# Weight-quarter sums of a Strassen product moved from GpSimd to VectorE, in three additions with changed signs

## The chip, the cores and the metric

The kernel runs on one core of a Trainium2 chip. The metric is the device time of one execution in microseconds, the median of the timed runs. The engines are named as the profile names them: PE is the matrix engine, TensorE (PEld its weight loads), DVE is VectorE, ACT is ScalarE, POOL is GpSimd, SP issues the transfers.

## The reference

Four residual layers work on x of 512 tokens by 1024 features, in float32. Layers 0 and 3 mix tokens with a gated short convolution, layer 1 with a spatial-gating unit (SGU), layer 2 with retention; each is followed by a SwiGLU feed-forward network (FFN) of 2816 hidden features, and a last RMSNorm closes.

```python
for i in range(4):
    h = rmsnorm(x, norm_mix_g[i])
    x = x + mixer[i % 3](h)                    # conv, SGU, retention, conv
    h = rmsnorm(x, norm_ffn_g[i])
    x = x + (silu(h @ w_gate) * (h @ w_up)) @ w_down
return rmsnorm(x, final_norm_g)

# the convolution mixer
b_gate, c_gate, z = split(h @ w_in, 3)
m = (b_gate * causal_conv3(c_gate * z)) @ w_out
```

## The kernel before

All activations lie with features on the 128 partitions and tokens along the row. Every float32 operand of a product is split into two float32r tiles whose sum it is (`split`, L156: ACT casts the high part, L157, then DVE subtracts it from the source to get the low part, L158), and a product is the three matmuls high by high, high by low, low by high (`product`, L177).

The products that read the residual stream in the convolution and FFN layers (`columns7`, L205) are made by Winograd's form of Strassen's product: weights and activations are cut into 2 by 2 quarters, and seven products of quarters or of sums of quarters take the place of eight. Each product is 12 matmuls of 256 columns, so a chunk of weights (two blocks of 128 output features) is 84 matmuls. Results are gathered from PSUM by short ACT copies (L227, L229, L233, L243) and DVE additions (`add`, L224).

`prepare7` (L114) makes the left operands of one chunk, in two halves of 512 KB each. For each half SP issues a transfer into a `raw` tile; the four sums of its quarters go into a `sums` tile, three of them by POOL in a chain (L131, L132, L133) and one by DVE (L134); then the three quarters that are used as they are, 128x768, and the four sums, 128x1024, are split by ACT and DVE. `weights` prepares at most one such chunk ahead of the one in use. `raw` has four buffers, `sums` two, the split weights four.

On the side of the activations, `operand_sums` (L382) makes the four sums of quarters for each pair of feature blocks: two by DVE (L391, L393) and two by POOL (L392, L394), then splits them (tiles th and tl). It runs once for each of the four pairs wherever a layer ends whose successor uses `columns7`. `operand` (L366) makes the plain parts xh and xl (L374, L375), and `squares` (L295) sums the squares of the new x on POOL (L302 to L307).

An FFN runs its hidden features in four parts. In a part of three pairs six chunks follow each other (gate, up, gate, up, ...; the tiles pg and pu), each 84 matmuls; within the next part's first pair the part's down projection (`leave`, L402) is added to x, eight blocks of 512-column matmuls. The first chunk of a layer is made by `columns4`, which needs no sums of the activations.

The order on each engine is made when the program is built, by a scheduler that simulates the engines; instructions marked urgent (`high_priority`) may pass up to 100 others. Each engine executes its own list strictly in that order.

Of the kernel before, what the change touches and what calls it, by code (L numbers as in the profile page):

```python
# [11 lines left out]
F32 = mybir.dt.float32  # L12
F32R = mybir.dt.float32r
# [4 lines left out]
P = 128  # L18
D = 1024
T = 512  # L20
DEPTH = 4
NB = D // P            # feature blocks of the residual stream
NT = T // P            # token blocks
FF = 2816
NF = FF // P
H = T // 2             # tokens of half the sequence
FF_PARTS = ((0, 2), (2, 5), (5, 8), (8, 11))  # pairs of hidden blocks, by part of an FFN
# [8 lines left out]
LAG = 3                # blocks of u that are ahead of the mixing of v  # L36
SOON = 100             # instructions that urgent ones may pass in the scheduler's order
BEGUN = 4              # blocks whose products begin before the last of their operands are ready
AHEAD = 4              # weight chunks prepared ahead of their matmuls


class Kernel:
# [19 lines left out]
    def dense(self):  # L62
        """Memory of the layers whose products take seven parts."""
# [10 lines left out]
    @contextmanager  # L74
    def mixed(self):
        """Memory of the other layers."""
        with self.tc.tile_pool(name="blk", bufs=29, reuse_waits="tile") as self.blk:
            yield

# [17 lines left out]
    def plan7(self, src, plain=False):  # L97
        """Two blocks of columns, for columns4 if plain, else for columns7."""
        self.chunks.append((src, 0, plain))
# [14 lines left out]
    def prepare7(self, i):  # L114
        """Two blocks of columns, as the seven left operands of Winograd's form of Strassen's product."""
# [3 lines left out]
        for half in range(2):  # L119
            raw = self.raw.tile([P, NB // 4, 4, P], F32, tag="raw", name=f"raw{i}{half}")  # L120
            nc.sync.dma_start(raw, src[half])
            if plain:
                h, l = (self.wp.tile([P, NB // 4, 4, P], F32R, tag=part, name=f"w{part}{i}{half}") for part in "hl")
                self.split(raw, h, l)
                for j in range(4):
                    out[j] += [(h[:, k, j], l[:, k, j]) for k in range(NB // 4)]
                continue
            sums = self.sums.tile([P, NB // 4, 4, P], F32, tag="sums", name=f"sums{i}{half}")
            a11, a12, a22, a21 = (raw[:, :, j] for j in range(4))
            s1, s2, s3, s4 = (sums[:, :, j] for j in range(4))  # L130
            nc.gpsimd.tensor_add(s1, a21, a22)  # L131
            nc.gpsimd.tensor_sub(s2, s1, a11)  # L132
            nc.gpsimd.tensor_sub(s4, a12, s2)  # L133
            nc.vector.tensor_sub(s3, a11, a21)  # L134
            for x, n, first, pool in ((raw, 3, 0, self.w7), (sums, 4, 3, self.wp)):
                h, l = (pool.tile([P, NB // 4, n, P], F32R, tag=part, name=f"w{part}{i}{half}{n}") for part in "hl")
                self.split(x[:, :, :n], h, l)
                for j in range(n):
                    out[first + j] += [(h[:, k, j], l[:, k, j]) for k in range(NB // 4)]
# [15 lines left out]
    def split(self, src, h, l):  # L155
        """A float32 tile as two float32r tiles whose sum it is."""  # L156
# [9 lines left out]
    def product(self, ps, terms, first=True, last=True, more=False):  # L166
        """ps (+)= sum of lhsT.T @ rhs over (lhs_h, lhs_l, rhs_h, rhs_l), the last term's at the end;
        more: added to a finished sum."""
# [12 lines left out]
    def columns(self, name, acts):  # L181
        """One block of output features (on partitions), for all tokens."""
# [14 lines left out]
    def begin(self, name, acts):  # L197
        """The start of columns(), with the weights of the rest."""
# [5 lines left out]
    def columns7(self, name, then, hold=False):  # L204
        """Two blocks of output features of the residual stream. then() gets them as [P, 2 * T], when the  # L205
        next product is under way."""
# [21 lines left out]
        part(c5, 3, xt, 0, True)  # L228
# [3 lines left out]
        part(c1, 4, xt, 1, False)  # L232
# [5 lines left out]
        part(c1, 5, xt, 2, False)  # L238
        add(y[:, 2 * H : 3 * H], c1, m5)

        def end():
            part(c1, 2, xt, 3, False)
            nc.scalar.copy(y[:, 3 * H :], c1)  # L243
# [4 lines left out]
    def columns4(self, name, then, hold=False):  # L248
        """The same by four products of blocks, for which the sums of the operand needn't be ready."""
# [16 lines left out]
    def finish(self, hold=False):  # L266
        """The rest of the last columns7, and what is done with its outcome (and those before it) unless on hold."""
# [8 lines left out]
    def rows(self, name, acts):  # L276
        """512 output features for each block of tokens (on partitions)."""
# [17 lines left out]
    def squares(self, src, add=None):  # L295
        """Running sum, over feature blocks, of the squares."""
# [12 lines left out]
    def rsqrt(self, ps, out, t):  # L309
        """out = ps ** -0.5, with a Newton step."""  # L310
# [7 lines left out]
    def scale_of(self, mean, r, t, *sums):  # L318
        """Each token's 1 / rms, on all partitions."""
# [8 lines left out]
    def diagonal(self, eye):  # L328
        """The matrix that mean_d is the inverse of, on vectors: D on the diagonal."""
# [8 lines left out]
    def scale_of_tokens(self, total):  # L338
        """Each token's 1 / rms, with tokens on partitions: a column for 128 of them."""
# [12 lines left out]
    def spread(self, r, t):  # L352
        """The same on all partitions, in PSUM."""
# [7 lines left out]
    def scale_in_psum(self):  # L361
        """Each token's 1 / rms, on all partitions."""
        return self.spread(self.scale_of_tokens(self.sum), self.hid.tile([P, 2 * T], F32, tag="hid", name="rs")[:, :T])

# [1 line left out]
    def operand(self, m, g):  # L366
        """x's block m as a part of the next product's operand."""
# [592 lines left out]
```

## Time and profile before

| what | value |
|---|---|
| median of 3 runs | 2485.07 us (2484.79 to 2485.66) |
| span of the profiled execution | 2484.2 us |
| PE busy | 2417.6 us, 97% |
| DVE busy | 1836.7 us, 74%, 2236 instructions |
| ACT busy | 1132.3 us, 46% |
| POOL busy | 890.0 us, 36%, 788 instructions |

The span runs from the first to the last instruction of one profiled execution. No separate time of that execution is given beside its span; the median of the timed runs is 0.9 us above it. A busy share is an average over stages with different limits: the seven-part stages (convolution and FFN) and the SGU and retention layers between them load DVE and POOL quite differently.

### The profile page before, as it was taken

Reading aid. Unit: us, or ns where it says so; the run is one execution under the profiler, and the core shown is the slowest. Engines: PE = TensorE matmul, PEld = TensorE weight load, DVE = VectorE, ACT = ScalarE, POOL = GpSimd, SP = SyncE. Lnnn points to the kernel's source line nnn. Section 1 sums busy time; section 2 is a strip of 40 time slices with the busy share of each in tenths; the row PEclk is TensorE's granted clock in tenths of the full one; section 3 lists DMA queues with packets and bytes.
Section 4 is the critical chain, followed back from the end, with each engine's and each line's share of the span. In section 5 each row is a group of like instructions: output and inputs, shape, how many; then the busy total and the mean of one; then the engine's idle time right before and its main releaser. Section 6 shows DMA issues by size and latency. Waiting matters only on the chain.

```text
span 2484.2 us, 37622 instructions
## 1 busy us (share of the span) xinstructions
PE 2417.6 (97%) x14892; PEld 2179.7 (88%) x14892; DVE 1836.7 (74%) x2236; ACT 1132.3 (46%) x1638; POOL 890.0 (36%) x788
## 2 busy tenths in 40 slices
PE   7999999999999999999999999999999899999998
PEld 6988989988888899998888888799999788889988
DVE  7988878763757887767565465988767898978776
ACT  6455445443324544534333334545435545545443
POOL 5536533520101643442000000834433744733530
PEclk9999999999999999999999999999999999999999
DMA  4141333334332233233223131233234124133231
GB/s 154 62 145 53 116 111 95 97 115 119 94 103 92 68 111 122 88 97 122 95 72 94 60 123 58 91 107 115 85 98 132 52 69 153 52 119 103 85 112 59
DMA packets 78832, 242.09 MB, mean 97 GB/s; under 512 B 8768, under 2 KB 12864, under 8 KB 78656
## 3 DMA queue, kind: packets, MB, share of 16 engines
q1 hardware_dynamic: 77568, 238.65, 30.3%
q8 instruction: 116, 1.90, 0.3%
q10 hardware_dynamic: 1088, 1.05, 0.1%
q14 instruction: 60, 0.49, 0.1%
HBM read 237.56 MB, written 2.10 MB: 96 GB/s over the span
## 4 chain that ended last, share of the span: by engine, by line
PE 75%; DVE 16%; issue 5%; ACT 2%; POOL 1%; DMA 0%; SPq 0%; DVEq 0%; ACTq 0%; POOLq 0%
PE out L177 26%; PE pu L177 16%; PE pg L177 15%; PE pv L177 7%; DVE wl L158 6%; PE pc L177 2%; PE q L177 2%; PE k L177 2%; PE pb L177 2%; DVE sums L134 2%; DVE puy L512 1%; PE pz L177 1%; DVE xl L375 1%; PE po L177 1%; DVE pgy L488 1%
## 5 line engine op out<-in xcount | busy, mean ns | idle before, releaser
L157 ACT CAST wh<-raw 128x768 fp32r<-128x768 f32 (+3 forms) x500 | 425.1, 858 | 572.5 <-PE out L177 193.5
L158 DVE TENSOR_TENSOR wl<-raw,wh 128x768 fp32r<-128x768 f32 (+3 forms) x500 | 557.6, 1134 | 136.7 <-ACT wh L157 136.3
L131 POOL TENSOR_TENSOR sums<-raw 128x256 f32<-128x256 f32 x208 | 243.3, 1170 | 795.8 <-DMA raw<-in_ffn_w_up 360.7
L157 ACT CAST wh<-sums 128x1024 fp32r<-128x1024 f32 x208 | 212.2, 1046 | 182.6 <-POOL sums L133 78.0
L177 PE MATMUL out<-hidl,wh 128*128 128x512 f32 (+1 forms) x736 | 278.3, 380 | 0.0
L158 DVE TENSOR_TENSOR wl<-sums,wh 128x1024 fp32r<-128x1024 f32 x208 | 260.9, 1279 | 22.1 <-ACT wh L157 18.8
L177 PE MATMUL out<-hidh,wh 128*128 128x512 f32 (+1 forms) x736 | 274.6, 381 | 0.0
L133 POOL TENSOR_TENSOR sums<-raw,sums 128x256 f32<-128x256 f32 x208 | 230.1, 1107 | 10.4
L132 POOL TENSOR_TENSOR sums<-sums,raw 128x256 f32<-128x256 f32 x208 | 217.9, 1048 | 10.6
L177 PE MATMUL pg<-xl,wh 128*128 128x256 f32 (+1 forms) x672 | 201.9, 316 | 9.6 <-DVE xl L375 9.6
L422 DVE TENSOR_TENSOR x<-out,x 128x512 f32<-128x512 f32 x192 | 130.2, 683 | 107.0 <-PE out L177 105.9
L177 PE MATMUL out<-hidh,wl 128*128 128x512 f32 (+1 forms) x736 | 205.4, 380 | 0.0
L177 PE MATMUL pg<-xh,wh 128*128 128x256 f32 (+1 forms) x672 | 200.9, 315 | 0.0
L177 PE MATMUL pu<-tl,wh 128*128 128x256 f32 x704 | 185.4, 284 | 5.1 <-DVE tl L158 5.1
L177 PE MATMUL pu<-xl,wh 128*128 128x256 f32 (+1 forms) x656 | 190.0, 306 | 0.0
L177 PE MATMUL pu<-xh,wh 128*128 128x256 f32 (+1 forms) x656 | 189.7, 306 | 0.0
L134 DVE TENSOR_TENSOR sums<-raw 128x256 f32<-128x256 f32 x208 | 153.3, 752 | 44.1 <-DMA raw<-in_ffn_w_up 37.9
L177 PE MATMUL pu<-th,wh 128*128 128x256 f32 x704 | 185.5, 285 | 0.0
L177 PE MATMUL pg<-th,wh 128*128 128x256 f32 x640 | 168.3, 284 | 6.9 <-DVE pgy L224 6.9
L177 PE MATMUL pg<-tl,wh 128*128 128x256 f32 x640 | 167.3, 283 | 0.0
L177 PEld LDWEIGHTS out<-hidl,wh 128*128 128x128 f32 x736 | 138.6, 188 | 25.1
L177 PEld LDWEIGHTS out<-hidh,wh 128*128 128x128 f32 x736 | 137.8, 188 | 25.0
(261 smaller groups left out, 6064.5 us busy)
## 6 DMA issues: line engine op xcount, KB each, us to landing
raw<-in_ffn_w_gate SPq DMA_DIRECT2D x88, 512.0 KB, 3.6
raw<-in_ffn_w_up SPq DMA_DIRECT2D x88, 512.0 KB, 3.6
raw<-in_ffn_w_down SPq DMA_DIRECT2D x96, 384.0 KB, 3.3
raw<-in_conv_w_in SPq DMA_DIRECT2D x48, 512.0 KB, 3.7
raw<-in_sgu_w_v SPq DMA_DIRECT2D x16, 512.0 KB, 3.6
raw<-in_sgu_w_u SPq DMA_DIRECT2D x16, 512.0 KB, 3.5
raw<-in_sgu_w_out SPq DMA_DIRECT2D x16, 512.0 KB, 3.5
raw<-in_ret_w_qk SPq DMA_DIRECT2D x16, 512.0 KB, 3.6
```

The lines of the kernel that those rows point to most:

```text
L131: nc.gpsimd.tensor_add(s1, a21, a22)
L132: nc.gpsimd.tensor_sub(s2, s1, a11)
L133: nc.gpsimd.tensor_sub(s4, a12, s2)
L134: nc.vector.tensor_sub(s3, a11, a21)
L157: self.nc.scalar.copy(h, src)
L158: self.nc.vector.tensor_sub(l, src, h.bitcast(F32))
L177: nc.tensor.matmul(ps, x, y, start=first and i == 0, stop=last and i == len(seq) - 1, skip_group_check=more)
L375: nc.vector.scalar_tensor_tensor(l[:, s], x[:, s], gm, h[:, s].bitcast(F32), ALU.mult, ALU.subtract)
L422: nc.vector.tensor_add(x[:, s], ps, x[:, s])
L488: self.nc.vector.tensor_mul(y, y, r.unsqueeze(1).broadcast_to([P, 2, T]))
L512: nc.vector.tensor_mul(y[:, s], y[:, s], g[:, s])
```

## The change

The signs of the sums are chosen so that all four sums of weight quarters are pure sums. They are made by DVE alone, in three additions: one of 512 columns that adds the fourth quarter, broadcast, to the first and third, and two of 256 columns that each add a quarter to the sum before. The opposite signs go to the activations: `operand_sums` makes its two chained sums on DVE as scalar_tensor_tensor instructions, and two results of `columns7` are negated where they are read out. The quarters lie one behind the other in a tile (the weights are laid out so in memory), and the slots of the four sums change their order. Comments are left out below.

```diff
-            raw = self.raw.tile([P, NB // 4, 4, P], F32, tag="raw", name=f"raw{i}{half}")
-            nc.sync.dma_start(raw, src[half])
...
-            sums = self.sums.tile([P, NB // 4, 4, P], F32, tag="sums", name=f"sums{i}{half}")
-            a11, a12, a22, a21 = (raw[:, :, j] for j in range(4))
-            s1, s2, s3, s4 = (sums[:, :, j] for j in range(4))
-            nc.gpsimd.tensor_add(s1, a21, a22)
-            nc.gpsimd.tensor_sub(s2, s1, a11)
-            nc.gpsimd.tensor_sub(s4, a12, s2)
-            nc.vector.tensor_sub(s3, a11, a21)
+            raw = self.raw.tile([P, 4, NB // 4, P], F32, tag="raw", name=f"raw{i}{half}")
+            sums = self.sums.tile([P, 4, NB // 4, P], F32, tag="sums", name=f"sums{i}{half}")
+            nc.sync.dma_start(raw, src[half])
+            nc.vector.tensor_add(sums[:, :2], raw[:, 3:].broadcast_to([P, 2, NB // 4, P]), raw[:, :3:2])
+            nc.vector.tensor_add(sums[:, 2], sums[:, 1], raw[:, 0])
+            nc.vector.tensor_add(sums[:, 3], sums[:, 2], raw[:, 1])
...
-        part(c5, 3, xt, 0, True)
+        part(c5, 4, xt, 0, True)
...
-        part(c1, 4, xt, 1, False)
+        part(c1, 5, xt, 1, False)
...
-        part(c1, 5, xt, 2, False)
-        add(y[:, 2 * H : 3 * H], c1, m5)
+        part(c1, 3, xt, 2, False)
+        with self.tc.high_priority(SOON):
+            nc.vector.scalar_tensor_tensor(y[:, 2 * H : 3 * H], c1, -1.0, m5, ALU.mult, ALU.subtract)
...
-            nc.scalar.copy(y[:, 3 * H :], c1)
+            nc.scalar.mul(y[:, 3 * H :], c1, -1.0)
...
-        nc.vector.tensor_sub(t1, b12, b11)
-        nc.gpsimd.tensor_sub(t2, b22, t1)
+        nc.vector.tensor_sub(t1, b11, b12)
         nc.vector.tensor_sub(t3, b22, b12)
-        nc.gpsimd.tensor_sub(t4, b21, t2)
+        nc.vector.scalar_tensor_tensor(t2, t1, -1.0, b22, ALU.mult, ALU.subtract)
+        nc.vector.scalar_tensor_tensor(t4, t2, -1.0, b21, ALU.mult, ALU.subtract)
```

In the changed program the lines below L115 stand one lower: the three additions of weight quarters are L132, L133 and L134, `operand_sums` is L392 to L395, the result with the changed sign is L240.

The change moves instructions at three places. The first is DVE's list within a part of the first FFN, from the split of one chunk's sums to the next chunk's. In the names the first two digits are the chunk, the next its half: wl5804 is the low part of the sums of half 0 of chunk 58, wl5803 that of its plain quarters. Before:

```order
L158 TENSOR_TENSOR wl5804_4107<-sums580_4097,wh5804_4106 128x1024
L158 TENSOR_TENSOR wl5814_4122<-sums581_4112,wh5814_4121 128x1024
L134 TENSOR_TENSOR sums590_4228<-raw590_4226 128x2x128
L134 TENSOR_TENSOR sums591_4243<-raw591_4241 128x2x128
L158 TENSOR_TENSOR wl5803_4103<-raw580_4095,wh5803_4102 128x768
L158 TENSOR_TENSOR wl5813_4118<-raw581_4110,wh5813_4117 128x768
L488 TENSOR_TENSOR pgy_4042<-pgy_4042,rps_2337 128x1024
```

And in the change, from the first addition for chunk 59 on:

```order
L132 TENSOR_TENSOR sums590_4181<-raw590_4180 128x512
L132 TENSOR_TENSOR sums591_4195<-raw591_4194 128x512
L158 TENSOR_TENSOR wl5803_4058<-raw580_4051,wh5803_4057 128x768
L133 TENSOR_TENSOR sums590_4181<-sums590_4181,raw590_4180 128x256
L158 TENSOR_TENSOR wl5813_4072<-raw581_4065,wh5813_4071 128x768
L489 TENSOR_TENSOR pgy_3998<-pgy_3998,rps_2313 128x1024
L133 TENSOR_TENSOR sums591_4195<-sums591_4195,raw591_4194 128x256
L224 TENSOR_TENSOR puy_4127<-pu2_4081,pum_4082 128x256
L134 TENSOR_TENSOR sums590_4181<-sums590_4181,raw590_4180 128x256
L224 TENSOR_TENSOR puy_4127<-pu5_4080,pum_4083 128x256
L134 TENSOR_TENSOR sums591_4195<-sums591_4195,raw591_4194 128x256
```

Two instructions for a chunk's sums have become six, and the two halves take turns, with other work between the links of each half's chain.

The second place is the end of DVE's list of the third FFN, where the activations for the second convolution are made after the last addition to x: xl2, xl3 and tl2, tl3 are the low parts for the last two pairs of feature blocks, xt their sums. Before:

```order
L375 SCALAR_TENSOR_TENSOR xl2_18033<-x2_90,gain_92,xh2_18032 128x512 x2
L134 TENSOR_TENSOR sums3121_18248<-raw3121_18246 128x2x128
L158 TENSOR_TENSOR tl2_18079<-xt_18071,th2_18078 128x1024
L391 TENSOR_TENSOR xt_18133<-xg_18132 128x256
L393 TENSOR_TENSOR xt_18133<-xg_18132 128x256
L375 SCALAR_TENSOR_TENSOR xl3_18107<-x3_91,gain_92,xh3_18106 128x512 x2
L158 TENSOR_TENSOR tl3_18141<-xt_18133,th3_18140 128x1024
```

In the change:

```order
L134 TENSOR_TENSOR sums3121_18100<-sums3121_18100,raw3121_18099 128x256
L395 SCALAR_TENSOR_TENSOR xt_17927<-xt_17927,xg_17926 128x256
L158 TENSOR_TENSOR tl1_17855<-xt_17847,th1_17854 128x1024
L376 SCALAR_TENSOR_TENSOR xl2_17889<-x2_90,gain_92,xh2_17888 128x512 x2
L392 TENSOR_TENSOR xt_17989<-xg_17988 128x256
L393 TENSOR_TENSOR xt_17989<-xg_17988 128x256
L394 SCALAR_TENSOR_TENSOR xt_17989<-xt_17989,xg_17988 128x256
L158 TENSOR_TENSOR tl2_17935<-xt_17927,th2_17934 128x1024
L395 SCALAR_TENSOR_TENSOR xt_17989<-xt_17989,xg_17988 128x256
L376 SCALAR_TENSOR_TENSOR xl3_17963<-x3_91,gain_92,xh3_17962 128x512 x2
L158 TENSOR_TENSOR tl3_17997<-xt_17989,th3_17996 128x1024
```

Between the last addition to x and tl3 DVE had 13 instructions and now has 21: the sums that POOL made (L394, L395) and the additions of weight quarters stand among them.

The third place is PE's list in the first convolution, at the matmul `scale` that sums the squares over the features (pc1 and pc2 are PSUM tiles of the products around it). Before, `scale` is row 153 of PE's list:

```order
L177 MATMUL pc2_466<-xh0_112,wh303_358 128x256
L344 MATMUL scale_496<-mean_d_94,sum_336 128x1 x4
L177 MATMUL pc2_466<-xl0_113,wh303_358 128x256
L177 MATMUL pc2_466<-xh1_119,wh303_358 128x256
L177 MATMUL pc2_466<-xl1_120,wh303_358 128x256
```

In the change it is row 208:

```order
L177 MATMUL pc1_460<-tl2_319,wh314_375 128x256
L177 MATMUL pc1_460<-th0_294,wl304_362 128x256
L345 MATMUL scale_492<-mean_d_94,sum_336 128x1 x4
L177 MATMUL pc1_460<-th1_306,wl304_362 128x256
L177 MATMUL pc1_460<-th2_318,wl314_376 128x256
```

The sum of squares is now asked for 55 rows of PE's list later, behind more products of 256 columns.

## Rows read from the trace of the kernel before

**Rows 1.** The page: span, and busy time of each engine.

```profile
span 2484.2 us, 37622 instructions
...
PE 2417.6 (97%) x14892; PEld 2179.7 (88%) x14892; DVE 1836.7 (74%) x2236; ACT 1132.3 (46%) x1638; POOL 890.0 (36%) x788
```

**Rows 2.** The waits view: engine, line waited for, us in total, times, longest.

```profile
ACT th L157 <- POOL xt L394: 31.3, 15, 3.8
...
PE pg L177 <- DVE xl L375: 9.6, 8, 2.8
...
PE pg L177 <- DVE pgy L224: 6.9, 9, 0.9
...
PE pu L177 <- DVE tl L158: 5.1, 3, 2.6
...
PE scale L344 <- DVE sum L307: 5.0, 1, 5.0
...
PE pc L177 <- DVE xl L375: 4.5, 3, 2.3
```

**Rows 3.** PE's timeline between two chunks of the first FFN: start, us, operation, idle before.

```profile
413.59 0.39 PE L177 MATMUL pg<-th,wh 128*128 128x256 f32 x1 [0.75 <-DVE pgy L224]
413.81 0.28 PE L177 MATMUL pg<-tl,wh 128*128 128x256 f32 x1
413.93 0.28 PE L177 MATMUL pg<-th,wh 128*128 128x256 f32 x1
```

**Rows 4.** DVE's timeline in the first FFN: start, us, operation, number joined.

```profile
360.20 0.42 DVE L134 TENSOR_TENSOR sums<-raw 128x256 f32<-128x256 f32 x1
...
362.77 0.96 DVE L158 TENSOR_TENSOR wl<-raw,wh 128x768 fp32r<-128x768 f32 x1
...
380.69 2.35 DVE L158 TENSOR_TENSOR wl<-sums,wh 128x1024 fp32r<-128x1024 f32 x2
382.96 1.85 DVE L134 TENSOR_TENSOR sums<-raw 128x256 f32<-128x256 f32 x2
384.74 2.90 DVE L158 TENSOR_TENSOR wl<-raw,wh 128x768 fp32r<-128x768 f32 x2
387.56 1.76 DVE L512 TENSOR_TENSOR puy<-puy,pgy 128x1024 f32<-128x1024 f32 x1
...
398.44 1.21 DVE L488 TENSOR_TENSOR pgy<-pgy,rps 128x1024 f32<-128x1024 f32 x1
...
402.24 1.22 DVE L158 TENSOR_TENSOR wl<-sums,wh 128x1024 fp32r<-128x1024 f32 x1
```

**Rows 5.** POOL's timeline in the same stretch, two rows of twelve.

```profile
383.72 0.81 POOL L132 TENSOR_TENSOR sums<-sums,raw 128x256 f32<-128x256 f32 x1
...
385.37 1.45 POOL L133 TENSOR_TENSOR sums<-raw,sums 128x256 f32<-128x256 f32 x1
```

**Rows 6.** DVE's timeline where the third FFN ends and the second convolution begins.

```profile
1918.65 0.68 DVE L422 TENSOR_TENSOR x<-out,x 128x512 f32<-128x512 f32 x1
1919.25 0.74 DVE L375 SCALAR_TENSOR_TENSOR xl<-x,gain,xh 128x512 fp32r<-128x512 f32 x1
...
1934.56 1.21 DVE L158 TENSOR_TENSOR tl<-xt,th 128x1024 fp32r<-128x1024 f32 x1
...
1940.32 1.51 DVE L134 TENSOR_TENSOR sums<-raw 128x256 f32<-128x256 f32 x1
...
1948.66 1.65 DVE L158 TENSOR_TENSOR tl<-xt,th 128x1024 fp32r<-128x1024 f32 x1 [0.57 <-ACT th L157]
```

**Rows 7.** The windows view: window, length, busy of PE, PEld, DVE, ACT, POOL, PEclk, DMA, GB/s.

```profile
51.00:57.00 6.00, 5.76 (x27) 5.79 (x28) 5.39 (x9) 0.96 (x3) 5.69 (x6) 0.50 0.01 2
1925.00:1975.00 50.00, 43.14 (x275) 38.26 (x274) 42.76 (x47) 30.20 (x45) 37.28 (x33) 0.97 0.14 43
1975.00:2080.00 105.00, 97.52 (x748) 93.38 (x747) 94.02 (x116) 48.83 (x83) 50.22 (x41) 1.00 0.29 93
```

**Rows 8.** Groups by line and form: busy, mean ns of one, idle before and its releasers.

```profile
L134 DVE TENSOR_TENSOR sums<-raw 128x256 f32<-128x256 f32 x208 | 153.3, 752 | 44.1 <-DMA raw<-in_ffn_w_up 37.9 <-DMA raw<-in_conv_w_in 5.0
```

More of the change, by code (lines that the diff above doesn't have):

```diff
@@ L119, in prepare7 @@
         for half in range(2):
-            raw = self.raw.tile([P, NB // 4, 4, P], F32, tag="raw", name=f"raw{i}{half}")
-            nc.sync.dma_start(raw, src[half])
             if plain:
-                h, l = (self.wp.tile([P, NB // 4, 4, P], F32R, tag=part, name=f"w{part}{i}{half}") for part in "hl")
+                raw = self.raw.tile([P, 4, NB // 4, P], F32, tag="raw", name=f"raw{i}{half}")
+                nc.sync.dma_start(raw, src[half])
+                h, l = (self.wp.tile([P, 4, NB // 4, P], F32R, tag=part, name=f"w{part}{i}{half}") for part in "hl")
                 self.split(raw, h, l)
                 for j in range(4):
-                    out[j] += [(h[:, k, j], l[:, k, j]) for k in range(NB // 4)]
+                    out[j] += [(h[:, j, k], l[:, j, k]) for k in range(NB // 4)]
                 continue
-            sums = self.sums.tile([P, NB // 4, 4, P], F32, tag="sums", name=f"sums{i}{half}")
-            a11, a12, a22, a21 = (raw[:, :, j] for j in range(4))
-            s1, s2, s3, s4 = (sums[:, :, j] for j in range(4))
-            nc.gpsimd.tensor_add(s1, a21, a22)
-            nc.gpsimd.tensor_sub(s2, s1, a11)
-            nc.gpsimd.tensor_sub(s4, a12, s2)
-            nc.vector.tensor_sub(s3, a11, a21)
+            raw = self.raw.tile([P, 4, NB // 4, P], F32, tag="raw", name=f"raw{i}{half}")
+            sums = self.sums.tile([P, 4, NB // 4, P], F32, tag="sums", name=f"sums{i}{half}")
+            nc.sync.dma_start(raw, src[half])
+            nc.vector.tensor_add(sums[:, :2], raw[:, 3:].broadcast_to([P, 2, NB // 4, P]), raw[:, :3:2])
+            nc.vector.tensor_add(sums[:, 2], sums[:, 1], raw[:, 0])
+            nc.vector.tensor_add(sums[:, 3], sums[:, 2], raw[:, 1])
             for x, n, first, pool in ((raw, 3, 0, self.w7), (sums, 4, 3, self.wp)):
-                h, l = (pool.tile([P, NB // 4, n, P], F32R, tag=part, name=f"w{part}{i}{half}{n}") for part in "hl")
-                self.split(x[:, :, :n], h, l)
+                h, l = (pool.tile([P, n, NB // 4, P], F32R, tag=part, name=f"w{part}{i}{half}{n}") for part in "hl")
+                self.split(x[:, :n], h, l)
                 for j in range(n):
-                    out[first + j] += [(h[:, k, j], l[:, k, j]) for k in range(NB // 4)]
+                    out[first + j] += [(h[:, j, k], l[:, j, k]) for k in range(NB // 4)]
         return out
@@ L880, in columns_by_two @@
     n, k, m = w.shape
-    w = w.reshape(n, 2, k // (4 * P), 2, P, m // (2 * P), 2, P).transpose(0, 5, 1, 4, 2, 6, 3, 7)
-    return np.ascontiguousarray(w.reshape(n, m // (2 * P), 2, P, k // (4 * P), 4, P)[..., [0, 1, 3, 2], :])
+    w = w.reshape(n, 2, k // (4 * P), 2, P, m // (2 * P), 2, P).transpose(0, 5, 1, 4, 6, 3, 2, 7)
+    return np.ascontiguousarray(w.reshape(n, m // (2 * P), 2, P, 4, k // (4 * P), P)[:, :, :, :, [0, 1, 3, 2]])
 def columns_first(w, parts=1):
```

## The prediction

> **What bounds the kernel now.** First the page: PE is busy for 97% of the span, DVE for 74%, POOL for 36% [rows 1]. The matmuls are the same before and after, so what can be won is PE's idle time and the stretches in which its clock is low, and what can be lost is new idle time. A matmul of 256 columns starts 0.12 us after the one before it [rows 3], so a chunk of 84 takes 10.08 us and a pair of chunks (gate and up) 20.16 us; no change of DVE or POOL makes that shorter.
>
> Next the waits. Those of PE that end with DVE are few [rows 2]: 9.6 and 4.5 us for the plain parts xl and 5.1 us for tl, all where a layer hands over to a layer of seven-part products; 6.9 us in nine pieces for pgy, within the FFNs; 5.0 us in one piece for the sum of squares at the first `scale`. Together 31.1 us. After the wait for `scale` the granted clock is 0.50, the lower level of 1.2 GHz, through 6 us [rows 7]: 3 us of PE's work at full speed are lost there. So 34 us is about all that faster handing over could give, and only the places of these waits matter.
>
> Then DVE's timeline, to see why it is late there. In the first FFN a pair of chunks takes DVE from 380.69 to 402.24, 21.55 us [rows 4], more than PE's 20.16. DVE falls behind by some 1.4 us a pair, and PE waits when the slack of a part is used up: the row of 0.75 us for pgy is that wait [rows 3]. DVE is slow there because of POOL. The addition of 256 columns takes 0.42 us when POOL rests and the split of 768 columns 0.96; while POOL works on sums [rows 5], two of the first take 1.85 and two of the second 2.90, and an addition of 1024 columns 1.76 where it takes 1.21 alone [rows 4]. The next operation starts about 0.08 us before the end of the one in front (2.35 for two splits that start 1.13 apart), so I count 0.34, 0.60, 0.88 and 1.13 us for 256, 512, 768 and 1024 columns: the 512 is from x's addition, which is followed after 0.60 us [rows 6]. A slowed operation costs (1.85 - 0.84) / 2, about 0.54 us more, counted at the starts: 0.89 for 0.34, 1.42 for 0.88.
>
> **The change, part by part.**
>
> *Weight sums in an FFN.* A pair holds two chunks, four halves. Removed per pair: twelve POOL additions, and with them the delay of four additions (4 x 0.55), four splits of 768 (4 x 0.54) and one of 1024 (0.55): 4.9 us. Added per half: one addition of 512 and two of 256 take the place of one of 256, 0.60 + 0.34 + 0.34 - 0.34 = 0.94 us, 3.8 us per pair. The two negated results become scalar_tensor_tensor instructions; on 512 columns that form takes 0.74 against 0.68 [rows 6], so 0.06 more, 0.1 per pair. The second and third addition of a half each wait for the one before. The order puts other work between most links, so a link costs nothing where it does and up to the 0.08 of overlap where it doesn't; two links in each of four halves bound that at 0.6. DVE's pair becomes 21.55 - 4.9 + 3.8 + 0.1 = 20.5, or 21.2 with all links exposed. At 20.5 it lags PE by 0.4 us a pair, 1.0 us over a part of three against 4.2 now, and the waits for pgy go: -6 of the 6.9 us (bounds 0 and -6.9; I take nearly all, since the order shown hides most links).
>
> *The VectorE price in the skill.* A single addition of 256 takes 0.42 us [rows 4] and of 512 takes 0.68 [rows 6]. The Trainium skill, "VectorE: DVE Perf Modes", section "The TRN2 errata — SBUF-src ops pay a fixed extra latency per instruction", gives (N + 151) / 0.96 ns, 0.42 and 0.69 us, as these rows do, and asks for few large instructions: it speaks against three small ones for one. Its section "The DRAIN you can't avoid" has the next operation start only when the pipe is empty. By that, a half's sums would cost 0.68 + 0.42 + 0.42, 1.52 us for my 1.28; the starts in [rows 4] stand closer than that for operations that don't depend on each other. What it makes of dependent ones is the second rival.
>
> *The first scale.* DVE makes the last sums of the first convolution's input before `scale`. It gets some eight scalar_tensor_tensor of 256 (0.40 each, 3.2 us) and part of five halves' additions (0.94 each, 4.7 us) before that point, and is rid of POOL's delays in a stretch where both are busy nine tenths of the time [rows 7]; `scale` itself stands 55 rows later, 6.6 us of matmuls at 0.12. So the sum may come later by 0 to 8 us and is asked for 6.6 us later. Bounds: nothing won, or the 5.0 us and the 3 us of low clock. I take the middle, -4.
>
> *The handing over to seven-part layers.* There are five such places (before the second convolution and the four FFNs), with 19.2 us of PE's waits together. In the one shown, DVE needs from the start of the first tl after the last addition to x, 1934.56, until the end of the last tl, 1950.31, 15.75 us [rows 6]. Its 13 instructions alone would take 4 x 1.13 + 5 x 0.34 + 4 x 0.66 = 8.9: the other 6.9 us are delays by POOL and waits for it, as the slowed rows (1.51 for 256 columns, 1.65 for 1024) show, and ACT waits 31.3 us in all for POOL's xt [rows 2]. Afterwards 21 instructions stand in the same place, 12.1 us alone: eight more, the chained sums and weight additions. POOL keeps only `squares` there, four of some ten operations in the stretch. If the delay shrinks with them, 12.1 + 2.7 = 14.8; if none of it goes, 19.0; if all goes, 12.1. So -3.6 to +3.2 each; I take -1 each, -5 together, with the proportional case. PE's clock sags there too (0.97 over 50 us), which gives nothing countable.
>
> *The convolutions.* Within 105 us of the second one PE is idle for 7.5, DVE for 11 [rows 7]. Per half DVE is rid of 1.09 (one addition and one split) and gets 0.97, so hardly anything follows from DVE's work; ACT and POOL no longer form a chain over three POOL operations. -3 for both, with bounds 0 and -8.
>
> *At nothing:* `mul` for `copy` on ACT, which is 46% busy [rows 1]; if not hidden, the same instruction count at the same size. Transfers are the same bytes in the same number. The first addition now needs the transfer where POOL's did; DVE waits 44.1 us for `raw` before L134 as it is [rows 8], in stretches where PE has slack. The broadcast operand of the first addition costs nothing: an addition with a broadcast operand of 1024 (L488) takes 1.21 like any other [rows 4].
>
> Sum: -6 - 4 - 5 - 3 = -18. The profiled span is 2484.2, so 2466 after; the median of the runs lies 0.9 above the span: **2467 us**. About 0.2%, 5 us, is what a measurement of this kernel can tell from no change.
>
> **The rivals.**
>
> 1. *Slower: handing over.* `squares` alone does most of the delaying, and DVE's list of 21 instructions reaches 19.0 us and more where 15.75 was. It decides from the point where the time from the last x to the last tl exceeds 15.75. 3.2 us at each of five places is 16 us more; with FFNs and convolution unchanged, and `scale` 6 us too late for its new place, 2507; with half of these 2495. For it: POOL's L306 and L307 remain. Against: they are fewer than half of POOL's work there. 0.17.
>
> 2. *Links pay the full latency.* Each addition of a half waits out the one before it: 1.52 us per half and 0.08 lost for its neighbours, DVE's pair near 21.5 as now. The FFN keeps its waits, the rest is half: 2485 - 6 = 2479. The page "VectorE: DVE Perf Modes" says that of any operation ("The DRAIN you can't avoid"). The rows here can't show it for chains, since DVE has none before. 0.13.
>
> 3. *Larger gain.* With POOL nearly silent DVE gets ahead everywhere: the 31 us of waits and the 3 us of low clock shrink to a few, as do the idle 7.5 us in each convolution: 2447. For it: 31.3 us of ACT's waits for POOL's xt go. The Trainium skill, "SBUF — State Buffer", section "SBUF: two separate sides", says that an addition of two operands on VectorE and a reading operation on GpSimd exclude each other for a whole instruction; the rows show about 0.54 us, less than the 0.81 to 1.45 of POOL's instructions. By the page more would be freed. 0.15.
>
> 4. *Nothing to tell.* Gains in the FFN and losses at the handing over cancel: 2485. 0.13.
>
> **How the numbers follow.** The forecast has 0.42, with its own range of 2459 to 2476. Faster by over 0.2% are the forecast, the third and most of the second rival: 0.69. No change: the fourth and a little of the second, 0.14. Slower: the first, 0.17. The range from 2443 to 2490 takes in the third rival and the fourth, and leaves out most of the first and a little beyond the third.
>
> **What the profile after would show.** L132 to L134 on DVE near 0.68, 0.42 and 0.42 us, splits of 768 near 0.96, DVE's pair of the first FFN from 20.5 to 21.2; no or few waits of PE for pgy; at `scale` a wait of 0 to 3 us, and the low clock after it shorter; waits for xl and tl around 14 us; POOL's busy time down by the three lines of sums, and no wait of ACT for it. I am wrong if the time from the last addition to x to the last tl grows, if DVE's pair stays at 21.5, or if a new PE wait for wl appears because DVE makes sums later than POOL did.

## The result, and the profile after

The median fell from 2485.36 us to 2457.83 us (2457.2 to 2461.18), a ratio of 0.9891 with a 95% interval of 0.9877 to 0.9905: 27.5 us faster. The forecast was 2467 us, 18 us faster, in a range from 2443 to 2490. The profiled execution went from 2484.2 us [rows 1] to 2455.3, 28.9 us less, so the two traces show the whole difference.

The page after: span, then busy time of each engine.

```profile
span 2455.3 us, 37035 instructions
...
PE 2410.1 (98%) x14892; PEld 2174.7 (89%) x14892; DVE 1861.4 (76%) x2700; ACT 1143.3 (47%) x1638; POOL 156.4 (6%) x116
```

POOL lost 734 us of work, and DVE, which took it over, is busy only 25 us longer than in [rows 1], though its sums of weight quarters take 318 us where they took 153 [rows 8]: most of what it gained in instructions it had been spending on delays. Groups of DVE by line and form (busy, mean ns of one, idle before):

```profile
L158 DVE TENSOR_TENSOR wl<-raw,wh 128x768 fp32r<-128x768 f32 x320 | 304.4, 964 | 37.9 <-ACT wh L157 37.4
L132 DVE TENSOR_TENSOR sums<-raw 128x512 f32<-128x512 f32 x208 | 142.1, 694 | 27.9 <-DMA raw<-in_ffn_w_up 24.0 <-DMA raw<-in_conv_w_in 3.2
L134 DVE TENSOR_TENSOR sums<-sums,raw 128x256 f32<-128x256 f32 x208 | 90.2, 436 | 1.5
L133 DVE TENSOR_TENSOR sums<-sums,raw 128x256 f32<-128x256 f32 x208 | 85.8, 417 | 0.8
```

The three sums (L132, L133, L134) cost 694, 417 and 436 ns; an addition of 256 columns had a mean of 752 [rows 8]. DVE's timeline of a pair of chunks in the first FFN, the one that answers to [rows 4]:

```profile
370.32 2.35 DVE L158 TENSOR_TENSOR wl<-sums,wh 128x1024 fp32r<-128x1024 f32 x2
...
389.65 0.42 DVE L240 SCALAR_TENSOR_TENSOR puy<-pu,pum 128x256 f32<-128x256 f32 x1 [0.89 <-PE pu L177]
...
391.12 2.35 DVE L158 TENSOR_TENSOR wl<-sums,wh 128x1024 fp32r<-128x1024 f32 x2
```

The pair takes 20.80 us from 370.32 to 391.12, and 0.89 of it is DVE waiting for PE. Before, it took 21.55 us [rows 4], with no wait for PE in it and one of 0.46 us for ACT:

```profile
400.77 1.22 DVE L488 TENSOR_TENSOR pgy<-pgy,rps 128x1024 f32<-128x1024 f32 x1 [0.46 <-ACT pgy L501]
```

So DVE's own time for a pair went from 21.1 to 19.9 us, below the 20.16 that PE needs: now it is PE that sets the pace. PE's waits after:

```profile
PE pu L177 <- DVE tl L158: 5.7, 4, 2.4
PE pz L177 <- ACT th L157: 4.7, 1, 4.7
PE pb L177 <- ACT pbm L229: 4.2, 1, 4.2
...
PE pg L177 <- DVE xl L376: 2.4, 4, 1.3
...
PE pg L177 <- DVE pgy L240: 0.4, 1, 0.4
```

Against [rows 2]: the wait for pgy fell from 6.9 to 0.4, that for xl from 14.1 to 2.4, and the first `scale` waits no more; that for tl stayed, and two long single waits for ACT are new. The window that answers to the first of [rows 7] (window, length, busy of PE, PEld, DVE, ACT, POOL, PEclk, DMA, GB/s):

```profile
51.00:57.00 6.00, 6.00 (x53) 6.00 (x52) 4.49 (x11) 4.43 (x7) 0.00 (x0) 1.00 0.01 4
```

PE is full there and its clock granted in full, where it was 0.50.

To see where the time came from, take the start of the same matmul of PE's timeline (the 450th, the 1000th and so on; both traces hold 14892) in both traces, and compare the stretches between (a handing over is the place where a layer ends and a layer of seven-part products begins):

| stretch, by matmul | before, us | after minus before, us | forecast |
|---|---|---|---|
| until the 450th: start of the first convolution | 84.3 | -12.0 | -4 |
| 450 to 1000: rest of it | 79.9 | 0.0 | -1.5 |
| the five places of handing over (1000 to 1200, 4800 to 5100, 8900 to 9350, 11250 to 11400, 12350 to 12600) | 245.8 | -4.2 | -5 |
| the insides of the four FFNs, without the last part | 1048.1 | -9.5 | -6 |
| 11400 to 12350: second convolution | 136.5 | -2.4 | -1.5 |
| SGU, retention, and the last part of the last FFN | 874.7 | 0.0 | 0 |

Another 0.8 us lie ahead of the first matmul. The same division is used for the experiments.

### The profile page after: what moved, and what is told of

It is laid out like the page before. It is cut to its first block, busy times and chain, and to the rows that moved or that the text cites. A ratio compares the mean times of both kernels' runs of the same rounds, so it can differ in the third digit from the quotient of the medians.

```text
span 2455.3 us, 37035 instructions
## 1 busy us (share of the span) xinstructions
PE 2410.1 (98%) x14892; PEld 2174.7 (89%) x14892; DVE 1861.4 (76%) x2700; ACT 1143.3 (47%) x1638; POOL 156.4 (6%) x116
## 4 chain that ended last, share of the span: by engine, by line
PE 90%; DVE 6%; issue 2%; ACT 1%; DMA 1%; POOL 0%; DVEq 0%; SPq 0%; ACTq 0%; POOLq 0%
PE out L177 26%; PE pu L177 21%; PE pg L177 21%; PE pv L177 7%; PE pc L177 3%; PE pb L177 3%; PE pz L177 3%; PE q L177 2%; PE k L177 2%; DVE wl L158 2%; PE po L177 1%; DVE xl L376 1%; PE ps L657 1%; DVE x L423 1%; DVE tl L158 1%
## 5 line engine op out<-in xcount | busy, mean ns | idle before, releaser
L158 DVE TENSOR_TENSOR wl<-raw,wh 128x768 fp32r<-128x768 f32 (+3 forms) x500 | 491.1, 992 | 135.0 <-ACT wh L157 134.5
L157 ACT CAST wh<-sums 128x1024 fp32r<-128x1024 f32 x208 | 215.1, 1049 | 172.8 <-DVE sums L134 88.6
L158 DVE TENSOR_TENSOR wl<-sums,wh 128x1024 fp32r<-128x1024 f32 x208 | 250.9, 1220 | 13.4 <-ACT wh L157 9.3
L132 DVE TENSOR_TENSOR sums<-raw 128x512 f32<-128x512 f32 x208 | 142.1, 694 | 27.9 <-DMA raw<-in_ffn_w_up 24.0
L177 PEld LDWEIGHTS out<-hidh,wl 128*128 128x128 f32 x736 | 136.1, 188 | 26.4
L177 PE MATMUL pg<-xh,wl 128*128 128x256 f32 (+1 forms) x672 | 149.7, 314 | 0.0
L177 PE MATMUL pu<-xh,wl 128*128 128x256 f32 (+1 forms) x656 | 147.4, 304 | 0.0
```

What stands on the lines that cost most here:

```text
L132: nc.vector.tensor_add(sums[:, :2], raw[:, 3:].broadcast_to([P, 2, NB // 4, P]), raw[:, :3:2])
L157: self.nc.scalar.copy(h, src)
L158: self.nc.vector.tensor_sub(l, src, h.bitcast(F32))
L177: nc.tensor.matmul(ps, x, y, start=first and i == 0, stop=last and i == len(seq) - 1, skip_group_check=more)
```

## The experiments

The theory: DVE is late because POOL's additions delay DVE's operations beside them, and the change wins by taking these away. The rivals: what is won comes from shorter chains (no trip to POOL and back); from the later place of `scale`; or from fewer, larger instructions. All ratios are to the kernel before, on the same chip and timed beside it.

**Either half alone.** `operand_only` moves only the two chained sums of the activations:

```diff
-        nc.gpsimd.tensor_sub(t2, b22, t1)
+        nc.vector.tensor_sub(t2, b22, t1)
...
-        nc.gpsimd.tensor_sub(t4, b21, t2)
+        nc.vector.tensor_sub(t4, b21, t2)
```

> The kernel before with only the two chained sums of operand_sums moved from POOL to DVE, as plain subtractions; the weight sums stay on POOL and DVE as they were. If the gain comes from the delays that POOL's weight additions put on DVE, the FFNs keep their pgy waits (6.9 us) and DVE's pair of 21.55 us, and only the start and the handing over can win: 0 to 8 us, about 2480. If the gain came from the shorter chain at the handing over (no trip to POOL), most of the 27 us would be here: about 2462.

Measured 2484.0 us, 0.9993 (0.9984 to 1.0002): no difference that can be told. Its waits:

```profile
PE pg L177 <- DVE pgy L224: 6.0, 8, 0.8
...
PE scale L344 <- DVE sum L307: 3.4, 1, 3.4
```

The FFN waits are there, though ACT's wait for POOL's xt is gone. The chain over POOL in `operand_sums` was not what held PE.

Nor does the chain of the weight sums look shorter to what follows it. ACT, which casts the sums, waited 78.0 us for POOL's last sum before (and 19.0 for the one that DVE made), and waits 88.6 us for DVE's last sum after:

```profile
ACT wh L157 <- POOL sums L133: 78.0, 42, 5.6
```

```profile
ACT wh L157 <- DVE sums L134: 88.6, 41, 5.7
```

`weights_three` is the other half: the change, with these two sums on POOL as plain subtractions. It leaves out the change of sign that the products need, so its output is not the reference's.

```diff
-        nc.vector.scalar_tensor_tensor(t2, t1, -1.0, b22, ALU.mult, ALU.subtract)
-        nc.vector.scalar_tensor_tensor(t4, t2, -1.0, b21, ALU.mult, ALU.subtract)
+        nc.gpsimd.tensor_sub(t2, b22, t1)
+        nc.gpsimd.tensor_sub(t4, b21, t2)
```

> The changed kernel with the two chained sums of operand_sums put back on POOL (as its two subtractions of before; the signs of two of the activation sums then differ from what the products need, so the output is not the reference's). If the delays by POOL's weight additions were the matter, nearly all of the gain stays: the FFN part in full (8 us) and most of the start, 2460 to 2466. If the trip to POOL in operand_sums was, the gain falls to under 10 us: over 2475.

Measured 2449.62 us, 0.9856 (0.9841 to 0.9872). The whole gain comes with the weight sums, and 8 us more than the change has: with the activations' sums on DVE, as the change has them, it is slower. `negative_gain` makes the same placing with the signs that the products need:

```diff
+                nc.scalar.mul(self.negative, self.gain, -1.0)
...
-            nc.scalar.mul(xg[:, s], self.x[k][:, s], self.gain_of(g, 2 * k + b))
+            gm = g * NB + 2 * k + b
+            nc.scalar.mul(xg[:, s], self.x[k][:, s], (self.negative if b else self.gain)[:, gm : gm + 1])
...
-        nc.vector.tensor_sub(t3, b22, b12)
-        nc.vector.scalar_tensor_tensor(t2, t1, -1.0, b22, ALU.mult, ALU.subtract)
-        nc.vector.scalar_tensor_tensor(t4, t2, -1.0, b21, ALU.mult, ALU.subtract)
+        nc.gpsimd.tensor_sub(t2, b22, t1)
+        nc.vector.scalar_tensor_tensor(t3, b22, -1.0, b12, ALU.mult, ALU.subtract)
+        nc.gpsimd.tensor_sub(t4, b21, t2)
```

> The three weight additions on DVE as in the change, and operand_sums back on DVE and POOL with right signs: ACT scales the second block by the negated gain, so that POOL's two plain subtractions give the sums that the products need and DVE's t3 becomes a scalar_tensor_tensor. It should take the time of the run that put these sums back on POOL with wrong signs, 2449 to 2452, 7 us less than the change. If that run was fast only by its order of instructions, 2455 to 2460.

Measured 2451.95 us, 0.9857 (0.9843 to 0.9870), as expected of the placing.

**POOL's load given back.** `pool_dummy` lets POOL add beside the change's DVE chain:

```diff
+            void = self.small.tile([P, NB // 4, P], F32, tag="void", name="void", bufs=1)
+            nc.gpsimd.tensor_add(void, raw[:, 3], raw[:, 2])
+            nc.gpsimd.tensor_sub(void, void, raw[:, 0])
+            nc.gpsimd.tensor_sub(void, raw[:, 1], void)
```

> The changed kernel, and POOL makes three additions of 256 columns per half besides, from the same raw tile into a tile that nobody reads: DVE's chain stays, POOL's load of before comes back. If the slowing of DVE by POOL is what was removed, DVE's additions and splits take 0.5 us more again while DVE also makes all sums: DVE's pair of chunks becomes about 25 us, PE waits for it, and the kernel is slower than before by far, above 2520. If only the chain over POOL was the matter, POOL's idle load costs nothing: 2458 to 2462.

Measured 2569.98 us, 1.0342 (1.0326 to 1.0358), 112 us over the change. The weight sums and the activations' sums have no chain over POOL in it, so POOL's load alone costs time. The sums on DVE (L137 and L138 are the second and third addition):

```profile
L132 DVE TENSOR_TENSOR sums<-raw 128x512 f32<-128x512 f32 x208 | 189.3, 921 | 20.5 <-DMA raw<-in_ffn_w_up 18.3 <-DMA raw<-in_conv_w_in 1.5
L137 DVE TENSOR_TENSOR sums<-sums,raw 128x256 f32<-128x256 f32 x208 | 121.0, 586 | 0.8
L138 DVE TENSOR_TENSOR sums<-sums,raw 128x256 f32<-128x256 f32 x208 | 119.1, 575 | 1.4
```

Each is slowed, by 0.14 to 0.23 us in the mean. The time is lost where the expectation did not look: inside the FFNs 28 us are lost against the change, 42 at the handing over, and 42 at the start and in the convolutions. DVE's pair of chunks grew only to 21.4 us (412.52 to 433.90), not 25. One reason is that at times it is POOL that is held up: in that pair one of its additions takes 6.92 us, and at the start one takes 19.31, through all of which DVE's rows have their usual length:

```profile
20.67 19.31 POOL L134 TENSOR_TENSOR void<-raw 128x256 f32<-128x256 f32 x1 [18.82 <-DMA raw<-in_conv_w_in]
```

The first additions of `squares` stand behind it in POOL's list. ACT waits 15.3 us for them, DVE 16.1, and PE then 13.0 for ACT. So most of the 17.5 us that are lost at the start come from a chain over POOL after all, that of `squares`, and not from slower rows of DVE. Over the trace without its last 60 us, PE's waits grow from 31 to 104 us, and PE works for 72 us at 0.50 of its clock instead of 16, which takes 28 us more. POOL's reading of raw also holds its buffers longer; DVE's idle time before L132, most of it for raw, fell from 27.9 to 20.5 us, which speaks against a large part for that.

`pool_memset` has POOL write as often without reading:

```diff
+            void = self.small.tile([P, NB // 4, P], F32, tag="void", name="void", bufs=1)
+            for _ in range(3):
+                nc.gpsimd.memset(void, 0.0)
```

> The changed kernel, and POOL fills a tile of 256 columns three times per half (three writes without a read in the place of the three additions of the run with POOL's idle load). If what slows DVE is any work of POOL on memory, DVE's rows grow beside the fills and the time goes above 2480. If it is POOL's reading, nothing: 2457 to 2460.

Measured 2456.76 us, 0.9877 (0.9863 to 0.9890), the time of the change.

```profile
L135 POOL MEMSET void<- 128x256 f32 x624 | 195.0, 312 | 35.1
L132 DVE TENSOR_TENSOR sums<-raw 128x512 f32<-128x512 f32 x208 | 141.4, 692 | 26.9 <-DMA raw<-in_ffn_w_up 23.4 <-DMA raw<-in_conv_w_in 2.9
```

624 fills leave DVE's row of 694 ns as it is. The fills are shorter than additions (312 ns against over 1000 in the mean) and wait for no transfer, but 195 us of POOL's work cost nothing that can be told. That agrees with the Trainium skill, "SBUF — State Buffer", section "SBUF: two separate sides", where only a GpSimd operation that reads collides with VectorE's operations of two operands.

**The place of `scale` alone.** `scale_after` is the kernel before with one call later in the first pc product by `columns7`:

```diff
-        self.finish(hold)
+        first = self.next == 4
+        if not first:
+            self.finish(hold)
...
         add(y[:, 2 * H : 3 * H], c1, m5)
+        if first:
+            self.finish(hold)
```

> The kernel before with one thing moved: the first scale of the first convolution stands behind all six parts of the second pc product (row 212 of PE's list instead of 153), sums on POOL as they were. If the 8 to 12 us that the change won up to the second group of products come from the later place alone, this wins about 8 us too: 2477, with no wait of scale and no low clock there. If they come from DVE being rid of POOL, little is won: 2482 to 2486, as the products that scale leads to come later.

Measured 2483.81 us, 0.9988 (0.9980 to 0.9997): 3 us. It wins 5.9 us up to the 450th matmul and gives 5.3 back by the 1000th. In its own start PE still has a wait:

```profile
49.52 0.58 PE L177 MATMUL pc<-th,wh 128*128 128x256 f32 x1 [2.76 <-ACT pcm L227]
...
56.86 0.95 PE L348 MATMUL scale<-mean_d,sum 128*128 128x1 f32 x8
```

`scale` no longer waits, another operation does; without DVE's and ACT's work earlier, the later place mostly puts the wait off.

**Three additions or four.** `weights_four` is the kernel before with its four sums, signs and all, on DVE:

```diff
-            nc.gpsimd.tensor_add(s1, a21, a22)
-            nc.gpsimd.tensor_sub(s2, s1, a11)
-            nc.gpsimd.tensor_sub(s4, a12, s2)
+            nc.vector.tensor_add(s1, a21, a22)
+            nc.vector.tensor_sub(s2, s1, a11)
+            nc.vector.tensor_sub(s4, a12, s2)
```

> The kernel before with its four weight sums all on DVE, in four additions of 256 columns with the signs of before, and operand_sums as before on DVE and POOL. By starts of 0.34 us each a half costs 1.36 us against 1.28 for the three instructions: within 3 us of the run with three additions and operand_sums on POOL, about 2452. If every small addition pays its whole 0.42 us, a half costs 1.68, DVE's pair of chunks is near 21.5 again, and the time is 2460 to 2470.

Measured 2453.17 us, 0.9864 (0.9850 to 0.9877), against 2451.95 of `negative_gain`, with overlapping intervals. The new signs and the joined addition bring nothing that these runs tell apart; the engine does.

**No sums.** `no_sums` splits raw's quarters in the place of the sums:

```diff
-            nc.vector.tensor_add(sums[:, :2], raw[:, 3:].broadcast_to([P, 2, NB // 4, P]), raw[:, :3:2])
-            nc.vector.tensor_add(sums[:, 2], sums[:, 1], raw[:, 0])
-            nc.vector.tensor_add(sums[:, 3], sums[:, 2], raw[:, 1])
...
-            for x, n, first, pool in ((raw, 3, 0, self.w7), (sums, 4, 3, self.wp)):
+            for x, n, first, pool in ((raw, 3, 0, self.w7), (raw, 4, 3, self.wp)):
```

> The changed kernel without any weight sums: the four quarters as they are loaded are split in their place (the output is not the reference's). This is what the sums still cost on DVE. If DVE's additions are hidden behind PE except where layers hand over, 2450 to 2456. If DVE is still what PE waits for in places, 2440 or less.

Measured 2431.33 us, 0.9780 (0.9767 to 0.9794): 26.5 us below the change. Inside the FFNs it wins only 0.8 us over the change; 14.4 us lie at the handing over and 12.1 in the convolutions. The sums on DVE are hidden in the FFNs and not there.

**What POOL still does.** `squares_dve` puts the later additions of `squares` on DVE, `squares_all` its first two operations too:

```diff
-            nc.gpsimd.tensor_scalar_add(sq[:, T:], sq[:, T:], RMS_EPS * D / P)
-            nc.gpsimd.tensor_add(self.sum, sq[:, :T], sq[:, T:])
+            nc.vector.tensor_scalar_add(sq[:, T:], sq[:, T:], RMS_EPS * D / P)
+            nc.vector.tensor_add(self.sum, sq[:, :T], sq[:, T:])
...
-            add = add or nc.gpsimd
+            add = add or nc.vector
```

> The changed kernel with the additions of squares on DVE too, so that POOL adds hardly anything where layers hand over. If what POOL's squares still cost DVE there (0.5 us for each operation beside them) is more than their own 0.60 us each, faster: 2450 to 2456. If DVE's own work is what counts there, slower by up to 1 us for each layer: 2458 to 2466.

> The changed kernel with all of squares on DVE, its first two operations too, which POOL takes 2.5 and 1.4 us for where layers hand over. If POOL's work beside DVE costs more than DVE's own doing of it, as it did for the other additions of squares (11 us won), this wins again, by 1 to 3 us: 2444 to 2446. If not, 2447 or more.

Measured 2446.93 us, 0.9837 (0.9824 to 0.9850), and 2438.84 us, 0.9805 (0.9792 to 0.9819): 11 and 19 us below the change, the second more than expected. The low part xl, which DVE makes while POOL adds squares, in the change and then in `squares_all`:

```profile
L376 DVE SCALAR_TENSOR_TENSOR xl<-x,gain,xh 128x512 fp32r<-128x512 f32 x64 | 61.2, 976 | 8.4 <-ACT xh L375 8.4
```

```profile
L376 DVE SCALAR_TENSOR_TENSOR xl<-x,gain,xh 128x512 fp32r<-128x512 f32 x64 | 46.8, 748 | 5.6 <-ACT xh L375 5.6
```

748 is the price of that form alone [rows 6]. In the change ACT also waits for POOL's squares. The longest row of this kind holds three waits; `squares_all` has none:

```profile
ACT xg L388 <- POOL sum L308: 13.9, 3, 4.8
```

Two more runs fill in the table of what POOL keeps. `squares_all_pool_chain` is `negative_gain` with the edit of `squares_all`, and `weights_pool` is `operand_only` with it:

> All of squares on DVE, and the two chained sums of operand_sums on POOL (with the negated gain). If POOL alone beside DVE is useful where only these eight short operations of a layer are left on it, it keeps the 6 us that this placing won in the change: 2439 to 2442. If every operation on POOL beside DVE costs DVE as much as it saves, the two placings are equal now: 2444 to 2448.

> The kernel before with the two chained sums of operand_sums and all of squares on DVE: POOL keeps the weight sums alone. If the weight sums on POOL are what DVE suffers from, the FFNs keep their pgy waits (7 us) and DVE, with more of its own to do where layers hand over, wins little there: 2472 to 2486. If squares and the sums on POOL weighed as much as the weight sums, 2450 to 2465.

Measured 2451.16 us, 0.9858 (0.9844 to 0.9871), and 2471.68 us, 0.9942 (0.9928 to 0.9955). By stretches of PE's list, profiled runs, each minus before:

| POOL keeps | kernel | median, us | start | inside the FFNs | handing over |
|---|---|---|---|---|---|
| weights, chain, squares | before | 2485.36 | 0 | 0 | 0 |
| weights, squares | operand_only | 2484.0 | -3.2 | -0.9 | +1.6 |
| weights | weights_pool | 2471.68 | +1.1 | -0.5 | -13.6 |
| chain | squares_all_pool_chain | 2451.16 | -10.8 | -10.0 | -12.7 |
| chain, squares | negative_gain | 2451.95 | -10.4 | -9.0 | -7.4 |
| squares | the change | 2457.83 | -12.0 | -9.5 | -4.2 |
| nothing of these | squares_all | 2438.84 | -11.6 | -9.5 | -18.0 |

The last two columns separate. The FFNs win 9.0 to 10.0 us in every run of this table without weight sums on POOL and under 1 us in the others; the handing over wins most where `squares` leaves POOL, with the weight sums or without.

One result fits neither theory: the chain of the activations on POOL saves 6 us beside the squares (2451.95 against 2457.83) and costs 12 us without them (2451.16 against 2438.84), where its expectation was a gain or none. Part of the 19 us between the change and `squares_all` lies in two single waits for ACT, 4.7 and 4.2 us, whose likes in `squares_all` are 2.0 and 1.4. The longer comes where the second convolution begins:

```profile
1916.91 0.58 PE L177 MATMUL pz<-th,wh 128*128 128x256 f32 x1 [4.72 <-ACT th L157]
```

About half or more of both differences is PE's clock. PE works at 0.50, the lower level of 1.2 GHz, for 16.0 us in the change and 10.2 in `negative_gain`, for 18.6 in `squares_all_pool_chain` and 3.4 in `squares_all` (the last 60 us of each trace left out); with half of that time counted as lost, this makes 2.9 of the 6 us and 7.6 of the 12. In a window over the beginning of the second convolution, first of `squares_all`, then of `squares_all_pool_chain`, PE is busy 4.5 us less in the second, at 0.93 of the clock for 0.98:

```profile
1900.00:2000.00 100.00, 95.53 (x731) 91.66 (x730) 92.44 (x150) 54.80 (x87) 0.00 (x0) 0.98 0.22 68
```

```profile
1900.00:2000.00 100.00, 91.02 (x653) 86.61 (x652) 86.51 (x137) 50.59 (x78) 10.74 (x6) 0.93 0.21 65
```

The waits themselves differ by 3.2 and 6.3 us over these traces. The order of instructions is written anew by the scheduler for each kernel, and whether order or delay makes the waits that differ stays open.

## Why the prediction was right

The sign, the mechanism and the range held; the sum, -18, fell 9.5 us short. The 2457.83 us lie a little below the forecast's own range, 2459 to 2476, and nearly half way to the third rival's 2447.

**FFN, -6: right in kind, -9.5.** Splits of 768 columns at 964 ns, sums near 0.68, 0.42 and 0.42 and the end of pgy's waits came as forecast. DVE's pair at 20.80 lies between the forecast 20.5 and 21.2, but 0.89 of that is a wait for PE; its own 19.9 is shorter than forecast, mostly because the 21.55 that the sum started from held the 0.46 us of waiting for ACT and counted it as work. The term was taken from the wait rows, 6.9 us, and a wait costs PE more than its row: each of the nine gave back about 1.0 us of the stretch that it lies in, where its row shows 0.7 to 0.9. Behind the wait of 0.75 us in [rows 3], for one, the next matmul starts 0.22 us later, not 0.12.

**The first scale, -4: mis-sized, -12.0.** I counted at most 8 us, the wait and the low clock, and took half, for fear of DVE's added instructions. They were no burden: DVE, rid of POOL's delays, finished the sum of squares 0.9 us earlier than before (at 50.17 us of the trace against 51.09) though it had more to make, and no wait and no low clock is left. `scale_after` shows that the place alone brings 5.9 us up to the 450th matmul, and 3 in all; the runs with the weight sums on DVE and no idle additions on POOL bring 9.4 to 12.6 up to there. At nearly the same place of PE's list, behind 196 and 198 matmuls, `scale` waits 3.4 us in `operand_only` and 0.5 in `weights_four`. What I left out is the next group of products: between the 200th and the 450th matmul 3.9 us went. The kernel before has a wait for a low part of weights there, and the clock is low behind it, by PE's timeline and by the window around it, both of the kernel before:

```profile
87.25 0.39 PE L177 MATMUL pc<-xh,wl 128*128 128x256 f32 x1 [1.99 <-DVE wl L158]
```

```profile
75.00:92.00 17.00, 15.01 (x113) 14.80 (x112) 17.00 (x19) 8.59 (x14) 10.72 (x8) 0.90 0.29 95
```

1.99 us of wait and some 1.7 us at 0.90 of the clock over 17 us make the 3.9 nearly up. This wait stood in the list of PE's waits (2.2 us for wl in pc products), and I had not put it among the places that the change could reach.

**Handing over, -5: right in sum by luck, wrong in its step.** -4.2 together, but in order the five places gave +3.4, -4.9, -1.5, -1.5 and +0.3 where I had -1 each. The time that I used as the measure, from behind the last addition to x to the end of the last tl, grew from 15.75 to 16.93 us, where I had 14.8, and that it grows was one of my own signs of being wrong:

```profile
1910.77 1.72 DVE L158 TENSOR_TENSOR wl<-sums,wh 128x1024 fp32r<-128x1024 f32 x1
1912.41 1.48 DVE L134 TENSOR_TENSOR sums<-sums,raw 128x256 f32<-128x256 f32 x1
...
1918.63 3.02 DVE L376 SCALAR_TENSOR_TENSOR xl<-x,gain,xh 128x512 fp32r<-128x512 f32 x2 [0.52 <-ACT xh L375]
...
1925.86 1.84 DVE L158 TENSOR_TENSOR tl<-xt,th 128x1024 fp32r<-128x1024 f32 x1 [0.41 <-ACT th L157]
```

Two xl take 3.02 here and 1.40 where POOL rests, an addition of 256 takes 1.48 for 0.41. That is the first rival's mechanism: squares alone keep delaying DVE, and its condition, more than 15.75 us, was met. At this place it cost PE nothing: counted from the start of the 11250th matmul, the last addition to x comes 2.5 us earlier than before and the end of the last tl 1.3 us earlier. The handing over to the first FFN is 3.4 us longer than before, and 0.1 in `squares_all`. The step that failed is the proportional delay, which left 2.7 us for POOL's four operations of ten: the four rows shown are 3.8 us longer than such rows alone, and some 1.2 us more are waits. The clock, which I put at nothing here, counted too: before, it is at 0.50 for 3.4 us at four of the five places, some 1.7 us lost at each; in the change it no longer falls at the second and third, and it is low twice as long at the fourth and newly at the fifth.

**Convolutions, -3: -2.4**, all in the second.

**The rivals.** Links at full latency (the second): a dependent addition starts 0.73 us behind its source where an independent one starts 0.60 behind it, by this piece of the change's DVE timeline, 0.04 after the source's end:

```profile
1931.03 0.69 DVE L132 TENSOR_TENSOR sums<-raw 128x512 f32<-128x512 f32 x1
1931.76 0.43 DVE L133 TENSOR_TENSOR sums<-sums,raw 128x256 f32<-128x256 f32 x1
```

An exposed link costs 0.13 us, not the 0.08 I bounded it with. The rule of the Trainium skill, "VectorE: DVE Perf Modes", section "The DRAIN you can't avoid", that the next operation does not start until the pipe is empty, agrees with the trace for dependent operations and not for independent ones. The same section adds that an operation that is not held starts earlier, which the prediction left out. In the list most links have other work between them. The larger gain (the third, 2447) was nearly as close as the forecast: the waits did shrink to a few, but squares remained, and `squares_all` at 2438.84 is that case and more. No change (the fourth) needed losses at the handing over that cancel the gains, and in sum there were none.

## What to carry to other kernels

Before you move work to an idle engine, look at what the busy engine's rows cost while it runs: here 734 us of POOL's additions beside DVE cost about as much of DVE's time as doing them on DVE (25 us less). Read it from the spread of one form's durations (0.42 us for one addition and 1.85 for two of them in [rows 4]), and where it shows, move the work back piece by piece, stage by stage: the weight sums paid in the FFNs, the squares where layers hand over. Compare traces by the start of the same matmul, since wait rows name only the last of several causes and leave out the low clock behind them.

## What the hardware showed that was not expected

POOL's fills of 256 columns beside DVE cost nothing (2456.76 us with 624 of them), its additions 112 us (2569.98 with as many), a part of them in POOL's own list. The delay goes both ways: an addition of 256 columns on DVE took 1.48 us beside POOL's squares and 0.41 alone, and one on POOL 19.31 us beside a busy DVE, where the next took 0.73. And even `squares`, 58 operations in the whole kernel, cost 19 us on POOL: putting them on DVE, at 0.69 us a piece for most, took the kernel from 2457.83 to 2438.84, the fastest run in which nothing is left out.
